# Zero-padded operands over all rows of the array, and weight chunks of half the size, in a two-block transformer kernel

## The chip, the core and the metric

The kernel runs on one core of a Trainium2 chip. A core has a matrix engine (TensorE, in the profile PE for its products and PEld for its loads of the stationary operand), VectorE (DVE), ScalarE (ACT), GpSimd (POOL) and SyncE (SP, which here only issues transfers). TensorE multiplies a stationary operand of up to 128 rows by 128 columns with a moving one of up to 512 columns. The metric is the device time of one execution in microseconds; lower is better.

## The reference, cut to what matters

Two transformer blocks of two layers each work on 512 tokens of 1024 features in float32. The first block has two SwiGLU feed-forward steps around a mixer of sliding-window attention (8 query heads, 2 key heads, window 128) and a convolution. The second block has a mixer of three parts (a gated delta rule, native sparse attention, stick-breaking attention) and a convolved feed-forward step. What the change touches are three products:

```python
# first block, sliding-window attention
s = jnp.einsum('bnqkgd,bnskd->bnkgqs', qb, kk) * (hd ** -0.5)
# second block, native sparse attention, selected and window keys
s_s = jnp.einsum('bqgrd,bgqnd->bgrqn', qb, k_sel) * scale
s_w = jnp.einsum('bqgrd,bngd->bgrqn', qb, kw) * scale
# second block, gated delta rule: q, k scaled per token
q = l2norm(to_chunks(q)) * D ** -0.5
k_beta = k * beta[..., None]
decay = jnp.exp(jnp.where(incl, g[..., :, None] - g[..., None, :], -jnp.inf))
```

A head has 64 features, so one head's queries or keys fill 64 of 128 partitions.

## The kernel before, in words

Activations are kept transposed: features on the 128 partitions, the 512 tokens along the columns. To keep float32 accuracy with the array's faster number format, each operand is split into a high and a low part, and a product of two tiles is three products (`mm3`, lines 259 to 261): high x high, high weight x low input, low weight x high input.

Weights come as chunks, in the order of use. `_fetch` (line 220) issues, on SyncE's queue, the transfers of the chunk that is wanted and the next ones, up to the `RAWS` = 3 buffers; a chunk is `CHUNK` = 8 tiles of 128 x 128, 512 KB. `_split_upto` casts half a chunk at a time, four tiles, to the high part on ScalarE (line 232) and subtracts for the low part on VectorE (line 233), `AHEAD` = 2 halves ahead of the products. A raw buffer is free again when its last half is split. In the second block's `compress` two whole chunks are used as they are (`wraw`).

The plan runs steps one after another: per layer of the first block a feed-forward step, `mixer1`, a feed-forward step and a gated embedding; per layer of the second block `mixer2`, `ffnc` and a gated embedding. A planner orders each engine's instructions from the program order, and lets an instruction that is ready pass one that still waits for a buffer.

In `mixer1` the products of the input come first; each of four convolution tiles is written to memory and read back four times, shifted (lines 478 and 482, SyncE's queue), into one of two buffers whose first columns GpSimd fills (line 480). Then, by query tile n, `scores(n + 1)` and `values(n)` alternate, and steps of the convolution (line 521) run beside them. A query tile `qs` holds [high, low] of one head on its 128 partitions, the key tile `ks` [high, high]; one product over all 128 rows (line 545) gives high x high plus low x high. The keys' low part is a second product over the 64 rows of the head (line 546), with `kl`, one tile for both key heads. VectorE takes the masked minimum from the score bank (line 549).

`mixer2` has the same pair in `nsa` (lines 1277 and 1278, tiles `kss`, `kws` and `ksl`, `kwl`). Its units of work are written out: the scores of unit u, then the transposes (line 1292) and the value products (line 266) of unit u - 2, then steps of the side work: output projection `pw`, the delta rule's scan, the compressed branch. The stages before it (`Gdn.pre`, `inverse`, `sb`) run with the remaining input products beside them. `pre` builds per-token factors as eight rows on partitions 0, 32 and 64 onwards, and `rows` (line 1514) spreads a group of eight over the partitions by a product with a selector `sel` of eight rows.

Of the kernel before, what the change touches and what calls it, by code (L numbers as in the profile page):

```python
# [10 lines left out]
F32 = mybir.dt.float32  # L11
# [7 lines left out]
T = 512  # L19
# [4 lines left out]
CHUNK = 8  # L24
AHEAD = 2
RAWS = 3
# [23 lines left out]
BLK = 16  # L50
SUB_RATE = 0.35
# [4 lines left out]
LAG = 4  # L56
# [9 lines left out]
class Vecs:  # L66
    """Column directory of the per-partition vectors."""
# [41 lines left out]
def const_layout():  # L109
    v = Vecs()  # L110
    for nm, n in (("tri", 128), ("last", 128), ("inc", 64), ("lev", 5 * 64), ("blk", 64), ("sub", 64), ("eye", BLK), ("hones", 2), ("high", 1), ("low", 1),
                  ("sbs", 128), ("cmask", 512), ("cmpm", 128), ("cmpn", 128)):
        v.add(nm, n)
    return v


class Net:
# [16 lines left out]
    def phase(self, **tags):  # L134
        """Scratch: rotating [128, 512] tiles, so many of each tag. Phases nest."""
# [8 lines left out]
    def psum(self, **tags):  # L144
        """PSUM banks, so many of each tag; or the tags that one goes round."""
# [41 lines left out]
    def setup(self):  # L187
# [5 lines left out]
        for i in range(8):  # L193
            nc.sync.dma_start(self.h[i], self.A["xT"][i * 128:(i + 1) * 128])
            if i in (0, 2, 4):
                self._fetch(i // 2, 1)
# [9 lines left out]
    def weights(self, sources):  # L206
        """The [128, 1024] chunks of all weights, in the order of use."""
# [7 lines left out]
    def _fetch(self, c, n=RAWS):  # L215
        for x in range(c, min(c + n, len(self.chunks))):
            if x not in self.rawt:
                r = self.raw.tile([128, CHUNK * 128], F32, tag="raw", name="raw")
                for f in (slice(0, 512), slice(512, 1024)) if x == 0 else (slice(None),):
                    self.nc.sync.dma_start(r[:, f], self.chunks[x][:, f])  # L220
                self.rawt[x] = r

    def _split_upto(self, h):
        nc = self.nc
        while self.nsplit <= min(h, 2 * len(self.chunks) - 1):
            c, half = divmod(self.nsplit, 2)
            if not self.israw[c]:
                self._fetch(c)
                r = self.rawt[c][:, half * 512:half * 512 + 512]
# [7 lines left out]
    def w(self):  # L237
        """The next 128-column tile of the weights."""
        h, o = divmod(self.at, CHUNK // 2)
# [6 lines left out]
    def wraw(self, n):  # L246
        """The next n chunks of the weights as they are."""
# [15 lines left out]
    def mm2(self, out, l, r, **flags):  # L263
        """A narrow product in two halves of its rows, side by side in the array."""
# [9 lines left out]
    def lin(self, name, xs, tag="lin"):  # L274
        """The next product."""
# [6 lines left out]
    def lead(self, name, n, tag="lin", gain=None, norm=None, at=8, between=None):  # L282
        """The input of a step, its first products side by side, and the norm of the input."""
# [51 lines left out]
    def rstd(self, tiles, n, scale=1.0, adds=SQ_DVE):  # L335
        """1/sqrt(mean(x^2)+eps) over the features of x = scale * tiles: a row on every partition."""
# [17 lines left out]
    def rn(self, acc, n, scale=1.0):  # L354
        """By token, 1/sqrt of the mean over the partitions."""
# [59 lines left out]
    def rope_tables(self, pos, inv, sgn):  # L415
        """cos and signed sin of pos * inv, features on partitions."""
# [24 lines left out]
    def rope(self, ps, cos, sin, half, tag="q", tmp="t"):  # L441
        """ps * cos + swap(ps) * sin, the swap within each 32 partitions."""
# [9 lines left out]
    def mixer1(self, i):  # L452
# [7 lines left out]
        # taps by fours: their weights on the diagonals of [4 x 32, 32], a group of 32 features after the other  # L460
# [8 lines left out]
        for j in range(4):  # L469
# [6 lines left out]
            # the tile's groups of 32 features, 0 to 3 tokens late  # L476
# [19 lines left out]
        # in parts, stacked: [high, low] of a head against [high, high] of its keys  # L496
        H = (slice(0, 64), slice(64, 128))
        kl, ks, qs = self.t(F32R, "kl", "q"), [], []
        for g in range(2):
            y = self.t(F32R, "ks", "q")  # L500
            for r in range(2):
                nc.scalar.copy(y[H[r]], kr[H[g]])
            nc.vector.tensor_tensor(kl[H[g]], kr[H[g]], y[H[g]].bitcast(F32), OP.subtract)
            ks.append(y)
        for j in range(4):
# [7 lines left out]
        def conv(j):  # L513
            """The convolution of tile j on the tensor engine, four taps at a time."""
# [18 lines left out]
        def scores(n):  # L533
# [4 lines left out]
            for g in range(2):  # L538
                for j in range(4):
# [6 lines left out]
                    last = nc.tensor.matmul(ps[:, f], q[H[g], b], kl[H[g], k], start=False, stop=True)  # L546
# [102 lines left out]
    def ple(self, pT, gain, norm, last=False):  # L649
        """The gate's product, and beside it the tokens' rms-normalised projection with its gain."""  # L650
# [46 lines left out]
    def final_out(self, gain, out):  # L697
        """The last norm, by token."""
# [38 lines left out]
    def pace(self, inst, **rates):  # L737
        """Steps of the work that runs beside the current one, so many of each kind, but not ahead of
        the instruction of LAG calls before."""
# [11 lines left out]
    def sparse(self, cost):  # L751
        """Small products of a cost were issued: as many large ones belong beside them."""
# [7 lines left out]
    def fill(self, kind, n=1):  # L760
        """n steps of a kind, or all that are left."""
# [11 lines left out]
    def need(self, done, kind):  # L773
        """Steps of a kind until done."""
# [9 lines left out]
    def by_token(self, y):  # L784
        """PSUM: the tokens of y on partitions, [token, (block, feature)]."""
# [5 lines left out]
    def mixer2(self, i, fin):  # L791
# [4 lines left out]
        st = self.t(name="st", tag="cd")  # L796
        nc.scalar.dma_start(st, self.A["sel"])
        sel = self.tp.tile([128, T], F32R, name="sel", tag="sel")
        nc.gpsimd.tensor_copy(sel, st)
# [105 lines left out]
    def norm2_in(self, i, fin):  # L905
        """The input of the second block's mixer; after the first block, its last norm too."""
# [4 lines left out]
        def gates(gain):  # L911
            """Their few columns in four groups, each a fourth of the features."""
# [13 lines left out]
        def norm():  # L926
# [13 lines left out]
            # of the two norms together: (mean of the second's square + eps) / first's^2  # L940
# [9 lines left out]
    def rsqrt_ln(self, x, n, scale):  # L950
        """1/sqrt(scale * x + eps): exp of the logarithm, and one Newton step."""
# [10 lines left out]
    def head_norm(self, *args):  # L962
        """out = src / rms(src) over each 64 columns."""
# [16 lines left out]
    def to_mix(self, o, nt):  # L980
        """A token block, transposed."""
# [937 lines left out]
```

## Time and profile before

| | us |
|---|---|
| time, median of 3 runs | 3790.53 |
| lowest and highest of the runs | 3789.84, 3797.76 |
| span of the profiled execution, first to last instruction | 3791.1 |

The times are of whole executions. For the profiled one only its span is on record; it lies 0.6 us above the median of the runs, so 3791.1 us serves as its own time. In the profile, "busy" counts an engine's own instructions; a TensorE product is listed with its start and a modelled length, and since products overlap, its cost is read from one start to the next. In the operand column `64*128` is 64 rows by 128 columns of the array in use, `64x256` the moving operand. The granted clock is 1.00 at 2.4 GHz and 0.50 at 1.2 GHz.

### The profile page before, as it was taken

What the parts mean: (1) busy time and instruction counts of PE and PEld (TensorE: products, weight loads), DVE (VectorE), ACT (ScalarE), POOL (GpSimd) and SP (SyncE); (2) the same over time, 40 slices, a digit from 0 to 9 for tenths busy, and PEclk for the clock granted to TensorE, in tenths of its full rate; (3) what the DMA queues carried; (4) which work ended last, traced back from release to release, by engine and by line L of the source; (5) the groups of instructions that cost most, each with busy time, mean ns of one, the idle gap of its engine ahead of it and who ended that gap; (6) DMA issues with size and microseconds to landing.
All of it is one profiled execution on the core that took longest, in us unless ns stands there. A gap on an engine that the chain in (4) does not pass through costs nothing. (4 is left out here: it accounts for less than half of the span.)

```text
span 3791.1 us, 53948 instructions
## 1 busy us (share of the span) xinstructions
PE 3723.9 (98%) x20946; PEld 2919.5 (77%) x20946; DVE 2311.5 (61%) x4820; ACT 1563.9 (41%) x2974; POOL 147.2 (4%) x150
## 2 busy tenths in 40 slices
PE   9999999999999999999999999999999999999998
PEld 7888757888888885688887777778887777778887
DVE  5445556444743445753448876675667786676667
ACT  4233344333532334532345344553445344554345
POOL 1000000000100000100001000000001000000001
PEclk9999999999999998999999998999999999999999
DMA  3223312222322242122232111122323111122232
GB/s 132 99 95 101 106 40 89 95 100 95 100 95 100 95 127 64 52 98 100 95 100 94 68 40 68 40 100 95 100 95 134 51 40 62 46 90 100 95 100 84
DMA packets 97152, 329.85 MB, mean 87 GB/s; under 512 B 11008, under 2 KB 14976, under 8 KB 96896
## 3 DMA queue, kind: packets, MB, share of 16 engines
q1 hardware_dynamic: 90144, 311.96, 24.9%
q10 hardware_dynamic: 5472, 10.25, 0.8%
q0 software_dynamic: 1280, 4.20, 0.3%
q8 instruction: 164, 2.69, 0.3%
q14 instruction: 92, 0.75, 0.1%
HBM read 317.97 MB, written 8.39 MB: 86 GB/s over the span
## 5 line engine op out<-in xcount | busy, mean ns | idle before, releaser
L232 ACT CAST wH<-raw 128x512 fp32r<-128x512 f32 x1116 | 691.3, 620 | 1421.9 <-PE pgu L260 451.2
L233 DVE TENSOR_TENSOR wL<-raw,wH 128x512 fp32r<-128x512 f32 x1116 | 791.2, 710 | 590.4 <-ACT wH L232 558.2
L259 PE MATMUL pgu<-xH,wH 128*128 128x512 f32 x1408 | 549.5, 391 | 9.7 <-ACT wH L232 5.9
L260 PE MATMUL pgu<-xL,wH 128*128 128x512 f32 x1408 | 551.2, 391 | 6.1 <-DVE xL L313 6.1
L261 PE MATMUL pgu<-xH,wL 128*128 128x512 f32 x1408 | 550.7, 391 | 0.0
L259 PE MATMUL pd<-H,wH 128*128 128x512 f32 x1056 | 410.8, 389 | 0.0
L260 PE MATMUL pd<-L,wH 128*128 128x512 f32 x1056 | 410.8, 389 | 0.0
L261 PE MATMUL pd<-H,wL 128*128 128x512 f32 x1056 | 410.8, 389 | 0.0
L259 PEld LDWEIGHTS pgu<-xH,wH 128*128 128x128 f32 x1408 | 265.3, 188 | 65.2 <-ACT wH L232 5.9
L260 PEld LDWEIGHTS pgu<-xL,wH 128*128 128x128 f32 x1408 | 266.3, 189 | 62.2 <-DVE xL L313 6.7
L261 PEld LDWEIGHTS pgu<-xH,wL 128*128 128x128 f32 x1408 | 266.2, 189 | 55.4 <-DVE wL L233 0.2
L259 PE MATMUL pup<-xH,wH 128*128 128x512 f32 x704 | 274.8, 390 | 2.2 <-DVE h L895 1.2
L261 PE MATMUL pup<-xH,wL 128*128 128x512 f32 x704 | 274.0, 389 | 0.0
L260 PE MATMUL pup<-xL,wH 128*128 128x512 f32 x704 | 273.9, 389 | 0.0
L260 PEld LDWEIGHTS pd<-L,wH 128*128 128x128 f32 x1056 | 198.2, 188 | 41.1
L259 PEld LDWEIGHTS pd<-H,wH 128*128 128x128 f32 x1056 | 198.2, 188 | 41.1
L261 PEld LDWEIGHTS pd<-H,wL 128*128 128x128 f32 x1056 | 198.2, 188 | 41.1
L348 POOL TENSOR_TENSOR ssum<-ssum,sq 128x512 f32<-128x512 f32 x72 | 110.6, 1536 | 2674.7 <-ACT sq L347 2673.3
L259 PEld LDWEIGHTS pup<-xH,wH 128*128 128x128 f32 x704 | 132.1, 188 | 31.5 <-DVE h L895 2.0
L261 PEld LDWEIGHTS pup<-xH,wL 128*128 128x128 f32 x704 | 132.1, 188 | 27.6
L260 PEld LDWEIGHTS pup<-xL,wH 128*128 128x128 f32 x704 | 132.1, 188 | 27.1
L1344 DVE SCALAR_TENSOR_TENSOR y<-x,vecs,y 128x511 f32<-128x511 f32 (+1 forms) x176 | 131.3, 750 | 17.1 <-ACT y L1341 14.3
(568 smaller groups left out, 6108.0 us busy)
## 6 DMA issues: line engine op xcount, KB each, us to landing
raw<-ffn SPq DMA_DIRECT2D x395, 512.0 KB, 3.2
raw<-w_in SPq DMA_DIRECT2D x82, 512.0 KB, 3.2
raw<-w_out SPq DMA_DIRECT2D x40, 512.0 KB, 3.2
raw<-w_ple_gate SPq DMA_DIRECT2D x40, 512.0 KB, 3.2
away<-h ACTq DMA_DIRECT2D x16, 256.0 KB, 2.1
raw<-cmp SPq DMA_DIRECT2D x8, 512.0 KB, 3.3
h<-away POOLq DMA_DIRECT2D x16, 256.0 KB, 5.1
h<-xT SPq DMA_DIRECT2D x8, 256.0 KB, 6.5
```

Source lines behind the costliest of these rows:

```text
L232: nc.scalar.copy(H, r)
L233: nc.vector.tensor_tensor(L, r, H.bitcast(F32), OP.subtract)
L259: nc.tensor.matmul(ps, w[0], x[0], start=first, stop=False)
L260: nc.tensor.matmul(ps, w[0], x[1], start=False, stop=False)
L261: nc.tensor.matmul(ps, w[1], x[0], start=False, stop=last)
L348: (nc.vector if k >= adds else nc.gpsimd).tensor_tensor(acc, acc, q, OP.add)
L1344: nc.vector.scalar_tensor_tensor(y[:, s:], x[:, :T - s], w[:, f * 3 + tap:f * 3 + tap + 1], y[:, s:], OP.mult, OP.add)
```

## The change

- Each key head gets a low-part tile of its own with zeros in the other head's 64 partitions, filled by GpSimd, and the low-part products take all 128 rows of the query tile: the other 64 rows meet zeros.
- The factor rows are products over 96 rows: `sel` has five blocks of 128 columns with ones only in the rows of one factor, and the moving operand is the whole of `RS`. `sel` grows from 512 to 640 columns and comes in two transfers.
- A weight chunk is 4 tiles, 256 KB, in 4 buffers instead of 8 tiles in 3. A split takes a whole chunk. The transfers at the start follow one after each of the first four tiles of the input; `compress` takes four chunks.
- Scratch: one more tile for `mixer1`, two more for `mixer2`; of the five level masks of the triangular inverse only the one in use stays.
- Comments and doc strings are dropped.

```diff
-CHUNK = 8
+CHUNK = 4
-RAWS = 3
+RAWS = 4
+LEVELS = tuple(range(BLK.bit_length() - 1, 5))
...
-            if i in (0, 2, 4):
-                self._fetch(i // 2, 1)
+            if i < RAWS:
+                self._fetch(i, 1)
...
-                for f in (slice(0, 512), slice(512, 1024)) if x == 0 else (slice(None),):
+                for f in (slice(0, 256), slice(256, 512)) if x == 0 else (slice(None),):
...
-        while self.nsplit <= min(h, 2 * len(self.chunks) - 1):
-            c, half = divmod(self.nsplit, 2)
+        while self.nsplit <= min(h, len(self.chunks) - 1):
+            c = self.nsplit
             if not self.israw[c]:
                 self._fetch(c)
-                r = self.rawt[c][:, half * 512:half * 512 + 512]
+                r = self.rawt[c]
...
@@ mixer1
-        kl, ks, qs = self.t(F32R, "kl", "q"), [], []
+        kl, ks, qs = [], [], []
         for g in range(2):
-            y = self.t(F32R, "ks", "q")
+            y, low = self.t(F32R, "ks", "q"), self.t(F32R, "kl", "q")
+            nc.gpsimd.memset(low[H[1 - g]].bitcast(F32), 0.0)
             for r in range(2):
                 nc.scalar.copy(y[H[r]], kr[H[g]])
-            nc.vector.tensor_tensor(kl[H[g]], kr[H[g]], y[H[g]].bitcast(F32), OP.subtract)
+            nc.vector.tensor_tensor(low[H[g]], kr[H[g]], y[H[g]].bitcast(F32), OP.subtract)
             ks.append(y)
+            kl.append(low)
...
-                    last = nc.tensor.matmul(ps[:, f], q[H[g], b], kl[H[g], k], start=False, stop=True)
+                    last = nc.tensor.matmul(ps[:, f], q[:, b], kl[g][:, k], start=False, stop=True)
@@ mixer2
-        st = self.t(name="st", tag="cd")
-        nc.scalar.dma_start(st, self.A["sel"])
-        sel = self.tp.tile([128, T], F32R, name="sel", tag="sel")
-        nc.gpsimd.tensor_copy(sel, st)
+        sel = self.tp.tile([128, 640], F32R, name="sel", tag="sel")
+        for f in (slice(0, 512), slice(512, 640)):
+            st = self.t(name="st", tag="cd")[:, :f.stop - f.start]
+            nc.scalar.dma_start(st, self.A["sel"][:, f])
+            nc.gpsimd.tensor_copy(sel[:, f], st)
@@ nsa_split, keys (ks and kw)
-            low = d[nm + "l"] = self.t(F32R, nm + "l", "gs")
+            d[nm + "l"] = []
             for g in range(2):
-                y = self.t(F32R, nm + "s", "gs" if nm == "ks" else "v")
+                y, low = self.t(F32R, nm + "s", "gs" if nm == "ks" else "v"), self.t(F32R, nm + "l", "gs")
+                nc.gpsimd.memset(low[H[1 - g]].bitcast(F32), 0.0)
...
+                d[nm + "l"].append(low)
@@ nsa, scores
-            nc.tensor.matmul(ps, q[s, b], d[key + "l"][s, :w], start=False, stop=True)
+            nc.tensor.matmul(ps, q[:, b], d[key + "l"][g][:, :w], start=False, stop=True)
@@ compress
-            W = self.wraw(2)
+            W = self.wraw(4)
@@ Gdn.pre
-        def rows(p, base, blk, f=lambda x: x):
-            nc.tensor.matmul(p, self.sel[base:base + 8, blk], f(RS[base:base + 8]), start=True, stop=True)
+        def rows(p, which, f=lambda x: x):
+            nc.tensor.matmul(p, self.sel[:96, which * 128:which * 128 + 128], f(RS[:96]), start=True, stop=True)
...
-        nc.vector.tensor_tensor(kb, k, rows(N.pat("row"), 32, B), OP.mult)
+        nc.vector.tensor_tensor(kb, k, rows(N.pat("row"), 3), OP.mult)
...
@@ build
-                        with n.phase(cd=4, gq=5, gs=4, gp=12, gat=3, v=4), tc.tile_pool(name="sp2", bufs=1) as n.sp2:
+                        with n.phase(cd=4, gq=5, gs=6, gp=12, gat=3, v=4), tc.tile_pool(name="sp2", bufs=1) as n.sp2:
-                            with n.phase(q=14, qt=2, S=8, t=2, p=2, o=3, c=8, cp=4):
+                            with n.phase(q=15, qt=2, S=8, t=2, p=2, o=3, c=8, cp=4):
```

## Rows read from the trace of the kernel before

**Rows 1.** The profile's page, part 1: busy us (share of the span) xinstructions.

```profile
PE 3723.9 (98%) x20946; PEld 2919.5 (77%) x20946; DVE 2311.5 (61%) x4820; ACT 1563.9 (41%) x2974; POOL 147.2 (4%) x150
```

**Rows 2.** A down projection's products: stretch, length, busy us (xcount), clock, DMA share, GB/s.

```profile
720.50:779.50 59.00, 58.96 (x261) 48.84 (x262) 4.83 (x7) 1.00 0.28 97
```

**Rows 3.** Busy time by stretch: the four attention stages.

```profile
452.00:542.00 90.00, 88.85 (x596) 37.89 (x594) 39.89 (x158) 39.33 (x129) 0.21 (x2) 0.85 0.12 30
...
1457.00:1543.00 86.00, 84.75 (x594) 37.17 (x595) 39.41 (x157) 38.66 (x129) 0.21 (x2) 0.86 0.13 32
...
2306.00:2460.00 154.00, 152.98 (x1342) 107.27 (x1341) 93.45 (x308) 77.35 (x219) 1.10 (x5) 0.91 0.13 42
...
3188.00:3330.00 142.00, 141.19 (x1330) 101.00 (x1328) 91.50 (x307) 74.49 (x214) 1.09 (x5) 0.98 0.14 46
```

**Rows 4.** Order of time on TensorE (start us, us): full products, second block.

```profile
2192.42 0.34 PE L1182 MATMUL sbz<-SL,cr 128*128 128x384 f32 x1
2192.59 0.40 PE L1182 MATMUL sbz<-SHL,cr 128*128 128x256 f32 x2
2192.83 0.22 PE L1182 MATMUL sbz<-SH,cr 128*128 128x128 f32 x1
```

**Rows 5.** Order of time on TensorE: a score unit of the second block.

```profile
2386.81 0.34 PE L1277 MATMUL pss<-kss,q0s 128*128 128x384 f32 x1
2387.08 0.43 PE L1278 MATMUL pss<-ksl,q0s 64*128 64x384 f32 x1
2387.44 0.44 PE L1292 MATMUL ppt<-ident,S 128*128 128x128 f32 x2
```

**Rows 6.** Order of time on TensorE: scores of the first block.

```profile
490.20 0.38 PE L545 MATMUL sc<-ks,qs 128*128 128x256 f32 x1
490.51 0.38 PE L546 MATMUL sc<-kl,qs 64*128 64x256 f32 x1
490.82 0.39 PE L545 MATMUL sc<-ks,qs 128*128 128x256 f32 x1
```

**Rows 7.** Order of time on TensorE: factor rows of the delta rule.

```profile
2081.05 0.73 PE L1514 MATMUL row<-RS,sel 8*128 8x512 f32 x3
2081.71 0.50 PE L260 MATMUL pqkv<-xL,wH 128*128 128x512 f32 x1
2082.05 0.39 PE L261 MATMUL pqkv<-xH,wL 128*128 128x512 f32 x1
2082.37 0.49 PE L1514 MATMUL row<-RS,sel 8*128 8x512 f32 x1
2082.79 0.50 PE L259 MATMUL pqkv<-xH,wH 128*128 128x512 f32 x1
```

**Rows 8.** One line's instructions: count, duration ns min/median/max, first and last start us.

```profile
L546 PE MATMUL sc<-kl,qs x64: 322/382/579, 452.7 to 1516.2; 64*128 64x256 f32 x48, 64*128 64x128 f32 x16
...
L1278 PE MATMUL pss<-ksl,q0s x16: 323/435/579, 2306.7 to 3301.9; 64*128 64x128 f32 x4, 64*128 64x256 f32 x4, 64*128 64x384 f32 x4, 64*128 64x512 f32 x4
...
L1514 PE MATMUL row<-RS,sel x24: 383/496/501, 2081.0 to 3052.4; 8*128 8x512 f32 x24
```

**Rows 9.** Waits from 452 to 516 us: total us, times, longest us.

```profile
POOL u L480 <- PE pc L521: 137.6, 2, 112.2
...
PEld sc L545 <- DVE nm L549: 4.7, 5, 1.6
```

**Rows 10.** DMA issues: out<-in engine op xcount, KB each, median us to landing.

```profile
raw<-ffn SPq DMA_DIRECT2D x395, 512.0 KB, 3.2
```

**Rows 11.** Order of time on SyncE, which issues the weights, first mixer.

```profile
396.21 2.08 SPq L478 DMA_DIRECT2D um<-ca  x2
...
403.20 0.38 SPq L220 DMA_DIRECT2D raw<-w_in  x1
...
483.95 27.22 SPq L482 DMA_DIRECT2D u<-um  x8
```

**Rows 12.** Busy time by stretch: one spell at the lower clock.

```profile
455.00:482.00 27.00, 26.82 (x77) 10.38 (x77) 9.70 (x42) 10.42 (x41) 0.00 (x0) 0.50 0.00 1
```

More of the change, by code (lines that the diff above doesn't have):

```diff
@@ L110, in const_layout @@
     v = Vecs()
-    for nm, n in (("tri", 128), ("last", 128), ("inc", 64), ("lev", 5 * 64), ("blk", 64), ("sub", 64), ("eye", BLK), ("hones", 2), ("high", 1), ("low", 1),
+    for nm, n in (("tri", 128), ("last", 128), ("inc", 64), ("lev", 64 * len(LEVELS)), ("blk", 64), ("sub", 64), ("eye", BLK), ("hones", 2), ("high", 1), ("low", 1),
                   ("sbs", 128), ("cmask", 512), ("cmpm", 128), ("cmpn", 128)):
@@ L237, in w @@
     def w(self):
-        h, o = divmod(self.at, CHUNK // 2)
+        h, o = divmod(self.at, CHUNK)
         if o == 0:
@@ L1103, in compress @@
             for l in range(16):
-                wl = W[l // 8][:, (l % 8) * 128:(l % 8 + 1) * 128]
+                wl = W[l // CHUNK][:, l % CHUNK * 128:(l % CHUNK + 1) * 128]
                 o, f = (0, 2 * l) if l < 8 else (1, 16 + 2 * l)
@@ L1269, in scores @@
             g, r, w = hd // 3, hd % 3, (n + 1) * 128
-            s, b = slice(g * 64, g * 64 + 64), slice(n * 128, n * 128 + 128)
+            b = slice(n * 128, n * 128 + 128)
             if hd == 0:
@@ L1511, in pre @@
         yield
-        def rows(p, base, blk, f=lambda x: x):
-            nc.tensor.matmul(p, self.sel[base:base + 8, blk], f(RS[base:base + 8]), start=True, stop=True)
+        def rows(p, which, f=lambda x: x):
+            nc.tensor.matmul(p, self.sel[:96, which * 128:which * 128 + 128], f(RS[:96]), start=True, stop=True)
             return p
-        A, B = slice(0, 128), slice(256, 384)
         kb = self.kb[j]
-        nc.vector.tensor_tensor(kb, k, rows(N.pat("row"), 32, B), OP.mult)
-        nc.vector.tensor_tensor(k, k, rows(N.pat("row"), 64, A), OP.mult)
+        nc.vector.tensor_tensor(kb, k, rows(N.pat("row"), 3), OP.mult)
+        nc.vector.tensor_tensor(k, k, rows(N.pat("row"), 4), OP.mult)
         yield
         self.qe[j] = self.room[j][1]
-        nc.vector.tensor_tensor(self.qe[j], q, rows(N.pat("row"), 32, A), OP.mult)
-        nc.vector.tensor_tensor(q, q, rows(N.pat("row"), 0, A), OP.mult)
+        nc.vector.tensor_tensor(self.qe[j], q, rows(N.pat("row"), 2), OP.mult)
+        nc.vector.tensor_tensor(q, q, rows(N.pat("row"), 0), OP.mult)
         yield
@@ L1532, in pre @@
         yield
-        pg = rows(N.pat("pg"), 0, B)
+        pg = rows(N.pat("pg"), 1)
         dt = self.t(name="dt", tag="gd")
@@ L1537, in pre @@
         nc.scalar.activation(dt, dt, AF.Exp)
-        pe = rows(N.pat("pel")[:, :8], 0, B, lambda x: x[:, 63::64])
+        pe = rows(N.pat("pel")[:, :8], 1, lambda x: x[:, 63::64])
         self.egl[j] = N.sp2.tile([128, 8], F32, name="el", tag="el", bufs=3)
@@ L1560, in lev @@
         def lev(l):
-            return N.con2("lev")[:, l * 64:(l + 1) * 64].unsqueeze(1).to_broadcast([128, 8, 64])
+            return N.con2("lev")[:, (l - LEVELS[0]) * 64:(l - LEVELS[0] + 1) * 64].unsqueeze(1).to_broadcast([128, 8, 64])
         def gi(name):
@@ L1591, in inverse @@
         N.pace(step, **rates)
-        for l in range(BLK.bit_length() - 1, 5):
+        for l in LEVELS:
             p = gi("px")
@@ L1865, in host @@
     con("lev", np.concatenate([(r // (2 * m) == c64 // (2 * m)) & (r // m % 2 == 1) & (c64 // m % 2 == 0)
-                               for m in (1, 2, 4, 8, 16)], 1))
+                               for m in (2 ** l for l in LEVELS)], 1))
     con("blk", r // BLK == c64 // BLK)
@@ L1883, in host @@
     con("low", lower)
-    S = np.zeros((128, 512), np.float32)
-    for c, h in ((0, 0), (1, 1)):
-        for r in (0, 32, 64, 4, 36, 68):
-            S[r + h, c * 64:c * 64 + 64] = 1
-    for c, h in ((2, 0), (4, 0), (5, 1), (7, 1)):
-        for r in (2, 34, 6, 38):
-            S[r + h, c * 64:c * 64 + 64] = 1
+    S = np.zeros((128, 640), np.float32)
+    for which, row in enumerate((0, 2, 32, 34, 64)):
+        for h in range(2):
+            for r in (row + h, row + h + 4):
+                S[r, which * 128 + h * 64:which * 128 + h * 64 + 64] = 1
     A["sel"] = S
```

## The prediction, on record before the result

> **What bounds the kernel now.** I read the page's busy times first: TensorE is busy 98% of the span, VectorE 61%, ScalarE 41%, GpSimd 4% [rows 1]. A busy TensorE is not yet a TensorE at its peak, so the next view is the busy time by stretch. In a down projection of a feed-forward step 261 products of 512 columns fill 59.0 us, 0.226 us from start to start, at a granted clock of 1.00 [rows 2]. That is the kernel's dense pace: 59.0 / 261. The four attention stretches look different [rows 3]. TensorE is just as busy there, but the granted clock is 0.85, 0.86, 0.91 and 0.98, and no other engine is near its limit: VectorE has 40 of 90 us and 94 of 154 us. So in these stages, too, it is TensorE's order of work that sets the end, and a shorter order should show in the span.
>
> Then the order of time on TensorE, which gives the cost of one product as the distance from its start to the next start. Products that use all 128 rows, one behind the other, take 0.17 us at 384 columns (2192.42 to 2192.59) and 0.12 us at 256 (two from 2192.59 to 2192.83) [rows 4]. A low-part product of the second block has 64 rows. With it, the pair of 384 columns takes 2386.81 to 2387.08, 0.27 us, and 2387.08 to 2387.44, 0.36 us, though nobody waits for data there [rows 5]. In the first block's attention a string of pairs of 256 columns runs at 0.31 us per product, both ways (490.20, 490.51, 490.82) [rows 6]. So what costs time is the change between a product over 64 rows and one over 128: about 0.10 us (0.27 - 0.17) before the 64-row product and 0.19 us (0.36 - 0.17, 0.31 - 0.12) behind it. The factor rows, with 8 rows, show the same: 2082.05 to 2082.37 is 0.32 us, 0.09 over the pace, and 2082.37 to 2082.79 is 0.42 us, 0.19 over it [rows 7].
>
> **The change part by part.** *Second block's scores.* Line 1278 runs 96 times, in six groups of 16 by query and key tile, of which one is shown [rows 8]. Each becomes a product over all rows. It has as many columns, so it should cost its pace, and both changes vanish if its neighbours are full, as the transposes behind it are [rows 5]: 0.10 + 0.19 = 0.29 us, over 96 products 28 us. Where a value product or a product of the scan (64 columns or rows of the array) comes next, the array is changed there anyway and only the first 0.10 us is saved; if that were so everywhere, the gain would be 10 us. Most are followed by a transpose or a large product, since the order puts the transposes of two units earlier right behind the scores, so I take 21 us, about a quarter off the upper end, and keep 10 to 28.
>
> *First block's scores.* Line 546 runs 64 times [rows 8]. Inside a string both products of the pair lose 0.19 us, 0.38 us a pair, 24 us at most; where the convolution (32 columns of the array) or the values come next only 0.19 us, 12 us at least. Half and half gives 18 us. Here something else is late next: VectorE's masked minimum frees the score banks, and TensorE already waits 4.7 us for it in five places of one layer [rows 9]. I take a third off: 12 us, bounds 5 and 24. These strides are those at the higher clock; at the lower one the changes cost more, which the upper bound covers.
>
> *Factor rows.* Line 1514 makes 24 row products [rows 8]. One that stands alone saves 0.09 + 0.19 = 0.28 us. But three issued together take 0.66 us in all (2081.05 to 2081.71), that is 0.22 us each, because products over different rows of the array run beside each other; over all rows they take 3 x 0.226 = 0.68 us [rows 7]. So the grouped ones save about nothing. The Trainium skill, "TensorE: Matmul & The Clock Gate", section "Why this matters for your kernels", says of products with few rows that they should be laid on distinct row groups so that they run at once, which speaks against widening them; by that rule, with all 24 in pairs that share one product's time, widening them adds 12 x 0.226 = 2.7 us. The trace bears the rule out for the grouped rows only; the low-part products have no partner to run beside. With half of the 24 alone the term is 12 x 0.28 = 3 us, with bounds of -3 (all of them sharing) and 6 (all alone). The other products of this line are few and I count nothing for them.
>
> *What is added.* Two half-tile fills per first mixer and four per second one, twelve in all, on GpSimd, which is busy 4% [rows 1]; the keys that they complete also wait for two ScalarE copies and a VectorE subtraction, so I cost them at nothing. If that cover were gone, each first use of a key tile would wait; the third rival prices it. The selector gets a second small transfer and a second conversion on GpSimd at the start of each second mixer, long before its first use; the constants beside it shrink by four of five level masks. Nothing.
>
> *Weight chunks.* A chunk is 512 KB and lands 3.2 us after its issue [rows 10]. The casts and subtractions keep their shape of 512 columns, so ScalarE and VectorE do the same work. What changes is how far the loads run ahead: three chunks of eight tiles are 24 tiles, four chunks of four are 16. Four tiles are 12 products, 2.7 us at the dense pace, so 16 tiles are 10.9 us, and with a landing of at most 3.2 us over 7 us are to spare in the dense stages. The place to look at is the first mixer, where SyncE issues no weights from 396.21 to 403.20, 7.0 us, because the convolution's copies hold its queue [rows 11]. The shorter lead is worth 8 tiles, 5.4 us, so at worst each of the two layers starves for 5.4 us, 11 us in all; the lead of 10.9 us is longer than the hold, so I take 1 us.
>
> *The clock.* Half speed, 1.2 GHz instead of 2.4, held without a break from 455 to 482 [rows 12]. From the granted clocks of the four stretches the time at the lower level is 2 x (1 - clock) x length: 27, 24, 28 and 6 us, 85 us in all [rows 3]. At half speed 85 us cost 42 us at most. All four lie where the scores start with their narrow products. The last two are the same program on the same shapes, once with 28 us and once with 6, so the stage stands near the edge where the level changes. With the pauses gone the same columns pass in less time, which should bring the higher level sooner, but the first scores will also wait more for VectorE. I take 6 us, bounds -11 (the fourth as long as the third: half of 22) and 42.
>
> The sum: 21 + 12 + 3 - 1 + 6 = 41 us. The profiled execution spans 3791.1 us, within 1 us of the median of 3790.5, so 3791.1 - 41 = 3750 us.
>
> **The rivals.** *The clock comes back as well.* If the longest three low stretches shrink to the 6 us of the fourth, 61 us less at the lower level give 30 us instead of 6, and with full score terms the time is about 3791 - 66 = 3725, down to 3706. For it speaks the fourth stretch; against it, that the first mixer's two spells are alike (27 and 24 us) and start at the same place. The Trainium skill, the same page's Part 1, has activity release the throttle from a half-speed default, which would favour this one.
>
> *The gain goes into waits.* TensorE gets through the scores faster but then stands for VectorE's minimum and the exponentials; only the second half of the second block's stage, where the large products of the output projection lie between the scores, gives its share: 10 + 5 = 15 us, 3776. For it: the 4.7 us of waits [rows 9]. Against it: VectorE is busy less than two thirds of every one of these stretches [rows 3].
>
> *The fills stand behind a blocked queue.* GpSimd's fill of a convolution buffer waits up to 112.2 us for the convolution to free it [rows 9]. If the key fills are queued behind it, the first block's low-part scores cannot start before that buffer is free, when the copies into it go out at 483.95 [rows 11], instead of at 452.7 [rows 8]: up to 31 us in each of two layers, 62 us, less the 41, a time of about 3812. It decides from 21 us a layer. Against it: SyncE's order shows later weights issued ahead of the blocked copies [rows 11], so the order lets ready work pass.
>
> *It does nothing.* The time lies in the narrow products themselves and not in the change of rows: 3791. The full products of equal width at 0.12 and 0.17 us [rows 4] speak against it.
>
> **How the numbers follow.** Forecast, 25 to 60 us less: 0.62. Clock as well, 60 to 85 us less: 0.15. Into waits, 8 to 25 us less: 0.12. Nothing: 0.04. Slower by the fills, or by starving weights: 0.07. A measurement of this kernel can tell about 0.2%, 7.6 us, from no change. Faster: 0.62 + 0.15 + 0.12 = 0.89; same 0.04; slower 0.07. For the range I leave out the nothing and slower cases and the outer ends of the two beside the forecast: 3706 to 3777.
>
> **What the profile after would show.** Right: the pairs of rows 5 and 6 at 0.17 and 0.12 us a product, with 128 rows on both; the second block's score stages 9 to 13 us shorter each, the first's 5 to 9 us; casts that wait for TensorE and not for a load. Wrong: strides that stay at 0.3 us on full rows; score products waiting for VectorE by as much as they were shortened; GpSimd's fills late; a pause between products of the first mixer before 420 us; low-clock stretches longer than before. The largest doubt is the clock, then how much of the first block's 18 us VectorE lets through.

## The result, and the profile after

| | before | after |
|---|---|---|
| median of the runs, us | 3794.15 (4 runs, 3789.84 to 3799.39) | 3724.24 (4 runs, 3721.87 to 3727.08) |
| span of the profiled execution, us | 3791.1 | 3725.3 |
| mean granted TensorE clock | 0.984 | 0.993 |

The ratio is 0.982, 95% interval 0.9804 to 0.9836: faster by 1.8%. The median lies inside the range on record and 26 us below the predicted point of 3750. A second measurement of the same kernel, beside the experiments, gave 0.9815 (0.9794 to 0.9836).

Busy time, as in [rows 1]. TensorE stays at 98% and is busy 70 us less with the same 20946 products; GpSimd, with its fills, is busy 9 us more:

```profile
PE 3654.2 (98%) x20946; PEld 2902.1 (78%) x20946; DVE 2307.7 (62%) x4820; ACT 1563.1 (42%) x2974; POOL 155.9 (4%) x164
```

The four attention stages by stretch, with the columns of [rows 3]. They are shorter, and the clock has risen in each: from 0.85, 0.86, 0.91 and 0.98 to these.

```profile
452.00:528.00 76.00, 72.74 (x593) 32.59 (x594) 39.14 (x158) 38.33 (x130) 0.23 (x2) 0.96 0.16 37
1443.50:1518.00 74.50, 72.48 (x596) 32.94 (x594) 38.99 (x158) 38.16 (x128) 0.23 (x2) 0.93 0.16 38
2281.00:2411.00 130.00, 128.93 (x1337) 99.24 (x1336) 91.07 (x306) 76.64 (x217) 1.11 (x5) 1.00 0.17 50
3139.00:3266.00 127.00, 125.53 (x1329) 97.73 (x1329) 90.50 (x307) 74.90 (x214) 1.10 (x5) 1.00 0.19 51
```

The order of time on TensorE in the second block, for the unit of [rows 5]. The pair of 384 columns goes at 0.17 us for the first product and 0.18 for the second, against 0.27 and 0.36 before:

```profile
2346.45 0.34 PE L1283 MATMUL pss<-kss,q0s 128*128 128x384 f32 x1
2346.62 0.34 PE L1284 MATMUL pss<-ksl,q0s 128*128 128x384 f32 x1
2346.80 0.38 PE L1298 MATMUL ppt<-ident,S 128*128 128x128 f32 x2
```

The same view in the first block, for the string of [rows 6]. Both products of a pair start 0.12 us apart, against 0.31:

```profile
480.07 0.28 PE L548 MATMUL sc<-ks,qs 128*128 128x256 f32 x1
480.19 0.28 PE L549 MATMUL sc<-kl,qs 128*128 128x256 f32 x1
480.31 0.28 PE L548 MATMUL sc<-ks,qs 128*128 128x256 f32 x1
```

The factor rows, as in [rows 7]. Three together take 2058.81 to 2059.59, 0.78 us, which is more than the 0.66 of the 8-row form; the single one takes 0.34 instead of 0.42, and the product ahead of it 0.24 instead of 0.32:

```profile
2058.81 0.94 PE L1520 MATMUL row<-RS,sel 96*128 96x512 f32 x3
2059.59 0.40 PE L261 MATMUL pqkv<-xL,wH 128*128 128x512 f32 x1
2059.83 0.39 PE L262 MATMUL pqkv<-xH,wL 128*128 128x512 f32 x1
2060.07 0.50 PE L1520 MATMUL row<-RS,sel 96*128 96x512 f32 x1
2060.41 0.39 PE L260 MATMUL pqkv<-xH,wH 128*128 128x512 f32 x1
```

The waits of the first mixer's attention, 452 to 503 us, with the columns of [rows 9]. TensorE and its loads now wait 8.3 us for VectorE's minimum (5.6 and 2.7), against 5.8 before (4.7 and 1.1). GpSimd's blocked fill `u` is still there. The first line is of before, the others of after:

```profile
PE sc L545 <- DVE nm L549: 1.1, 1, 1.1
```

```profile
POOL u L481 <- PE pc L524: 123.7, 2, 101.5
...
PEld sc L548 <- DVE nm L552: 5.6, 5, 1.9
...
PE sc L548 <- DVE nm L552: 2.7, 3, 1.8
```

GpSimd's order of time. The two key fills come at 371.97, a hundred microseconds ahead of the fill of 474.53, whose wait for the convolution stands in its bracket. So the key fills wait behind nothing:

```profile
371.97 1.10 POOL L502 MEMSET kl<- 64x512 f32 x2
474.53 0.11 POOL L481 MEMSET u<- 128x12 f32 x1 [101.46 <-PE pc L524]
```

A chunk of half the size lands in 2.6 us, against 3.2 in [rows 10]:

```profile
raw<-ffn SPq DMA_DIRECT2D x791, 256.0 KB, 2.6
```

In the first mixer, where the lead was feared to be too short, ScalarE's casts do wait for a load:

```profile
412.50 1.27 ACT L233 CAST wH<-raw 128x512 fp32r<-128x512 f32 x2 [5.30 <-DMA raw<-w_in]
414.41 0.62 ACT L233 CAST wH<-raw 128x512 fp32r<-128x512 f32 x1 [0.64 <-DMA raw<-w_in]
```

TensorE filled that gap with 24 products of the convolution, which before stood a little later (at 416.50). The products of the next tile, `pk`, which come behind both, start at 419.46:

```profile
413.89 2.76 PE L524 MATMUL pc<-u,cd 128*32 128x512 f32 x24
...
419.46 0.39 PE L260 MATMUL pk<-xH,wH 128*128 128x512 f32 x1
```

Before, they started at 419.19. The starved loads cost 0.3 us at most in this layer.

### The profile page after: what moved, and what is told of

It reads as the page before. It is cut to its first block, busy times and chain, and to the rows that moved or that the text cites. A ratio compares the mean times of both kernels' runs of the same rounds, so it can differ in the third digit from the quotient of the medians.

```text
span 3725.3 us, 55291 instructions
## 1 busy us (share of the span) xinstructions
PE 3654.2 (98%) x20946; PEld 2902.1 (78%) x20946; DVE 2307.7 (62%) x4820; ACT 1563.1 (42%) x2974; POOL 155.9 (4%) x164
```

## The experiments

Stage lengths below go by the first product of one kind to the first of another: the first mixer from `pag` to `pA`, the score stage of the second block from `pss` to `pup`. "Low" is time at 1.2 GHz inside the stage.

Three theories. One: the change from 64 rows to 128 and back costs the time, and strings of such changes also go with the low clock. Two: it is the half-filled array during the low-part products that goes with the low clock, and the number of changes does not matter for it. Three: the spells at the low clock come by chance, and the wide score products give only their direct time.

**Both blocks' low products on 64 rows, the rest of the change kept.**

```diff
-last = nc.tensor.matmul(ps[:, f], q[:, b], kl[g][:, k], start=False, stop=True)
+last = nc.tensor.matmul(ps[:, f], q[H[g], b], kl[g][H[g], k], start=False, stop=True)
...
-nc.tensor.matmul(ps, q[:, b], d[key + "l"][g][:, :w], start=False, stop=True)
+nc.tensor.matmul(ps, q[s, b], d[key + "l"][g][s, :w], start=False, stop=True)
```

> The changed kernel with only the low-part score products of both blocks put back on the 64 rows of their head; padded tiles, chunks and factor rows stay. Theory 1 (each change between 64 and 128 rows stops the array, and the stops bring the clock down): the strides of 0.31 us return, the low-clock time in the four attention stages goes from 17 back to about 85 us, time 3785 to 3795 us, mean clock about 0.984. Theory 2 (the half-filled products, not the stops, bring the clock down) expects the same here. Theory 3 (the clock's spells are chance and only the strides changed): about 3755 us, clock between 0.984 and 0.993. If the smaller chunks had part in the gain, the time stays more than 8 us below the kernel before.

3773.79 us, ratio 0.9936 (0.9912 to 0.9961), clock 0.988. Of the 70 us gained 50 are gone by the medians and 44 by the ratios: the low clock of the first mixer is back (27 and 24 us), that of the second block's score stage is not (0 and 0). The time lies between the 3785 to 3795 of theories one and two and the 3755 of three; the low time is 51 us, not the 85 that the first two expected.

**Only the first block's on 64 rows** (the first of the two edits).

> Only the first block's low-part products back on 64 rows. Theories 1 and 2: the first block's two attention stages return to 90 and 86 us of length, from 76 and 75, so about 25 us above the changed kernel, 3750 us, with about 50 us of low clock there and none in the second block's score stages. Theory 3: about 9 us above, 3733 us.

3747.11 us, 0.9867 (0.9837 to 0.9897). The first mixers are back at 170.5 and 166.8 us, with 24 us of low clock in each; the score stages stay short, 153.5 and 152.7. The median fits the 3750 of theories one and two, but the profile is of the slowest of four executions, and the fastest, 3737.75 at a clock of 0.992, lies near the 3733 of theory three.

**An eight-column product of 64 rows ahead of each of the 160 wide pairs**, overwritten by the pair.

```diff
+nc.tensor.matmul(ps[:, f][:, 0:8], q[H[g], b], kl[g][H[g], k][:, 0:8], start=True, stop=True)
 nc.tensor.matmul(ps[:, f], q[:, b], ks[g][:, k], start=True, stop=False)
...
+nc.tensor.matmul(ps[:, 0:8], q[s, b], d[key + "l"][g][s, 0:8], start=True, stop=True)
 nc.tensor.matmul(ps, q[:, b], d[key + "s"][g][:, :w], start=True, stop=False)
```

> The changed kernel, with all low-part products on all rows, and ahead of each of the 160 score pairs one product more, of 64 rows and only 8 columns, whose output is overwritten: the changes of rows return without any half-filled work to speak of. At 0.10 us before and 0.17 us behind each, 30 to 43 us come directly. Theory 1: the clock falls as well, the low time in the attention stages rises from 17 to 60 us or more, time 3775 to 3800 us. Theory 2: the clock stays at about 0.993, time 3754 to 3767 us.

3784.86 us, 0.9967 (0.9953 to 0.9982), clock 0.987: 61 us above the changed kernel by the medians, 56 by the ratios, 57 by the spans of the profiles. The price of the change alone, on TensorE in the second layer's mixer:

```profile
1467.10 0.27 PE L548 MATMUL sc<-kl,qs 64*128 64x8 f32 x1
1467.30 0.39 PE L549 MATMUL sc<-ks,qs 128*128 128x256 f32 x1
1467.52 0.28 PE L550 MATMUL sc<-kl,qs 128*128 128x256 f32 x1
1467.73 0.27 PE L548 MATMUL sc<-kl,qs 64*128 64x8 f32 x1
```

The eight-column product takes 0.20 us to the next start (1467.10 to 1467.30), the wide product behind them takes 0.22 (to 1467.52) and the one ahead of the next eight 0.21 (to 1467.73), instead of 0.12 each. In this string a pair costs 0.63 us instead of 0.24, so the eight columns cost 0.39 in all. Elsewhere a neighbour is narrow anyway or TensorE waits for VectorE: with low time taken at the 0.41 us per us worked out below, the four attention stages are 41 us longer than the changed kernel's, 0.26 us for each of the 160. The other 15 to 20 us go with the clock (99 us of low time in the whole execution, against 57), though almost no column was added on half the rows. In the four stages the low time is 51 us, against 17; theory one had asked for 60 or more. All ten executions had a clock of 0.985 to 0.990. Theory two, with 0.993 and 3754 to 3767 us, falls.

**First block on 64 rows, ordered high, high, low, low within each score bank.** The same products are issued, but in this order the score sums are not the right ones (probably part of one head's sum in each bank is lost; no run shows it). So the run tells times and is no kernel to use.

```diff
+for _, _, f, q in pair:
+    nc.tensor.matmul(ps[:, f], q[:, b], ks[g][:, k], start=True, stop=False, ...)
+for _, _, f, q in pair:
+    last = nc.tensor.matmul(ps[:, f], q[H[g], b], kl[g][H[g], k], start=False, stop=True, ...)
```

> As first_back, but the two pairs of a score bank are issued as full, full, low, low, so that the 64-row products come two by two and half of the changes go. Theory 1: of the roughly 9 us that the changes cost directly about half comes back and the low-clock time falls with them: 8 to 14 us below first_back. Theory 2: as many half-filled columns as in first_back, so its low-clock time, and only 3 to 6 us below it.

3726.32 us, 0.9814 (0.979 to 0.9837): 21 us below the ungrouped form, more than theory one (8 to 14) and theory two (3 to 6) expected, and as fast as the wide products. On TensorE four products now take 0.86 us (1461.34 to 1462.20), 0.215 each, between the 0.31 of [rows 6] and the 0.12 of the wide form:

```profile
1461.34 0.50 PE L553 MATMUL sc<-ks,qs 128*128 128x256 f32 x2
1461.77 0.50 PE L555 MATMUL sc<-kl,qs 64*128 64x256 f32 x2
1462.20 0.50 PE L553 MATMUL sc<-ks,qs 128*128 128x256 f32 x2
```

128 products by 0.095 us are 12 us at most. All four executions had a clock of 0.992, and the ungrouped one that had it as well was 11 us slower (3737.75), so the direct part holds. The rest of the 21 goes with the clock: in the profiles the low time of the two first mixers fell from 48 to 17 us. Half the changes and the same number of half-filled columns speak for theory one; but two later profiles with ungrouped narrow scores have 14 and 3 us there, so this run alone does not decide between one and two.

**The changed kernel once more, and with the factor rows on 8 rows.**

> The changed kernel once more, unaltered, as the standard for the runs beside it on the same chip. It was 3724 us (3722 to 3727); the same within 5 us is expected, with the same 57 us of low clock within 15.

> The changed kernel with the delta rule's factor rows as products over 8 rows again, and nothing else altered. By the working on record the wide factor rows are worth 3 us (bounds -3 and 6), so 3 us above the changed kernel. The rival: three grouped 8-row products share the array's time, so the wide form gains nothing or loses up to 3 us, and this kernel is equal or up to 3 us faster. A third: the factor rows' changes of rows also hold the clock down, as the score products' do, and the low-clock spells near 2073 and 2107 us return (10 us at half speed, 5 us of time).

3722.7 us (0.9815) and 3729.62 us (0.9833, interval 0.9811 to 0.9854): 7 us, more than the 3 on record. The repeat met its expectation. The clock is not the answer: the low time of a whole execution is 57 us with 8 rows, and 57 and 65 in the two profiles with 96, whose spans lie only 2 to 3 us below. To find where, I added up over all factor products the time from the start of the product ahead to the end of the group, where the next product starts. The 24 of tile `row` take 10.7 us with 8 rows and 10.2 with 96: nothing to speak of. The twelve others of the same line, the decays `pg` and the eight-column `pel`, bring the sum for all 36 from 18.7 to 16.1 us. One of these with 8 rows, and one with 96:

```profile
2058.99 0.40 PE L261 MATMUL pqkv<-xL,wH 128*128 128x512 f32 x1
2059.32 0.27 PE L1519 MATMUL pel<-RS,sel 8*128 8x8 f32 x1
2059.52 0.50 PE L262 MATMUL pqkv<-xH,wL 128*128 128x512 f32 x1
```

```profile
2064.66 0.40 PE L261 MATMUL pqkv<-xL,wH 128*128 128x512 f32 x1
2064.89 0.18 PE L1520 MATMUL pel<-RS,sel 96*128 96x8 f32 x1
2064.93 0.48 PE L262 MATMUL pqkv<-xH,wL 128*128 128x512 f32 x1
```

0.53 us from the product ahead to the one behind against 0.27: the eight-column product saves as much as a lone one of 512 columns (0.74 against 0.47 in four of six places). So 2.6 us are direct, as the spans have it; the other four of the seven are near what these runs can tell, and I leave them open.

**Half-size chunks alone, on the kernel before.**

> The kernel before with the weight chunks of four tiles in four buffers, and nothing else of the change. If the clock in the second block's score stage hangs on the changes of rows alone, its low stretches there stay (27 and 7 us), the clock stays at 0.98, and the time is that of the kernel before, up to 2 us more. If the smaller chunks decide where that stage starts and so whether its spell comes, the stretches are gone as in the run with both blocks' low products on 64 rows, the clock is 0.988, and the time is 3775 to 3785.

3789.46 us, 0.9999 (0.9986 to 1.0012). The chunks cost nothing and bring nothing. The low time of the score stages is 10 us in each here, where the kernel before has 27 and 10, with no product changed.

**Wide factor rows alone, on the kernel before.**

> The kernel before with the wide factor rows and their longer selector, and nothing else of the change. Direct term: the stretch between the second block's first product and its score stage, with the low time taken at half, was 2.7 and 1.3 us longer with 8-row factor rows than without, so 4 us, a ratio of 0.999. If the factor rows' changes of rows also bring the low clock of the score stage behind them (27 and 10 us in the kernel before), that is gone too, another 10 to 17 us: a ratio of 0.995 and a clock 0.004 higher.

3781.87 us, 0.9977 (0.9964 to 0.9989): 9 us, between the two expectations. The low time of the score stages was 14 and 7 us, so it had not gone. This kernel also has the four level masks fewer, so the 9 us are not the factor rows' for certain.

**Scores and factor rows both narrow again** (chunks, zero-filled tiles and their room kept), **and the first experiment again beside it.**

> The changed kernel with the score products on 64 rows and the factor rows on 8 rows again: what is left of the change is the chunks, the zero-filled tiles and their room. Chunks alone gave a ratio of 0.9999, the run with only the score products back 0.9936. If the 24 us between these two are the factor rows' (directly and by the clock), this kernel gives 0.999 to 1.000 and the low stretches of the score stage return; if they come from the fills, the extra buffers or the order that follows from them, it gives 0.994.

> The run with only the score products on 64 rows once more, unaltered, as the standard for the two beside it: a ratio of 0.9936 within 0.002 and no low clock in the score stage, if the 24 us between it and the chunks alone are a property of the kernel; a ratio nearer to 1 if they were that execution's or that chip's.

0.9971 (0.996 to 0.9982) and 0.9947 (0.9933 to 0.9962). The repeat met its expectation (within 0.002, and 0 us of low time in both score stages). The kernel with both kinds narrow meets neither of its two: the factor rows account for 9 of the 24 us that were asked about (20 by the repeat), and about 10 remain in a kernel that has neither kind of wide product. One of its score stages had 38 us of low time, the other none. The repeat also shows how much of such a difference is one execution's. It is the program of the first experiment, and its 975 products of the second layer's first mixer took 166.78 us at a clock of 0.93 in one profile (first fence) and 158.47 us at 0.99 in the other (last row of the second fence; its first two rows are the score stages):

```profile
1376.94:1543.72 166.78, 165.53 (x975) 101.06 (x973) 90.19 (x257) 67.70 (x177) 1.41 (x6) 0.93 0.30 80
```

```profile
2292.36:2457.26 164.90, 160.58 (x1476) 118.02 (x1474) 112.05 (x343) 90.17 (x246) 8.34 (x15) 1.00 0.19 55
3163.58:3325.81 162.23, 157.75 (x1469) 116.71 (x1468) 111.24 (x343) 88.63 (x243) 7.83 (x10) 1.00 0.19 55
1372.35:1530.82 158.47, 157.17 (x975) 98.31 (x973) 90.18 (x257) 67.56 (x177) 1.41 (x6) 0.99 0.32 84
```

That is the price of the clock with nothing else in it: 2 x 0.07 x 166.78 - 2 x 0.01 x 158.47 = 20.2 us less at half speed bring 8.3 us, 0.41 us for each. The next pair gives the same.

**Half-size chunks and the scratch of the changed kernel, none of its wide products.**

> The run with the chunks alone, with the scratch of the changed kernel besides (one more tile in the first mixer, two more in the second, one level mask instead of five), without its zero-filled tiles, wide scores or wide factor rows. The run with everything but the wide products gave a ratio of 0.9971, the chunks alone 0.9999. If the 10 us between them come from the buffers (keys that wait for a free tile ahead of the score stage), this gives 0.997 and the clock 0.986; if from the filled tiles and the order that they bring, 0.9995 to 1.000 and 0.984.

3777.06 us, 0.9959 (0.9944 to 0.9975). Three more scratch tiles and four constants fewer are worth 15 us over the chunks alone. The same stage of the second layer, with chunks alone and then with the room:

```profile
1376.40:1543.20 166.80, 165.55 (x976) 101.19 (x974) 90.25 (x257) 67.86 (x177) 0.36 (x4) 0.93 0.30 80
```

```profile
1373.20:1531.60 158.40, 157.10 (x976) 98.41 (x974) 90.15 (x257) 67.56 (x177) 0.36 (x4) 0.99 0.32 84
```

TensorE issues the 975 products of this stage in the same order in both, reaches the first score after 81.1 us in both, and waits 1.1 us at the same place. The long low spell begins 4 us after the first score product in the one (1461.6) and not at all in the other, where a short one comes at 1470.0, 16 us after it. So it is not this order that the room changed. The twelve runs of this kernel went from 3769.42 us at a clock of 0.992 to 3797.9 at 0.981, the ten with chunks alone only from 0.986 down to 0.982. The ratio fits the expectation of 0.997 roughly, but its reason, keys that wait for a free tile, is not what the trace shows: around the head of the first score stage (2290 to 2340 us) TensorE waits 0.6 us in all with chunks alone, and not at all with the room. Whether it is the tiles or the masks no run separates.

**More products widened by zeros:** the stick-breaking scores, with a key tile per head, and the compressed branch's second value product.

```diff
-nc.tensor.matmul(p, d["sk"][j][s, b * 128:(b + 1) * 128], d["sq"][j][s, b * 128:], start=True, ...
+nc.tensor.matmul(p, d["sk"][j][hd % 2][:, b * 128:(b + 1) * 128], d["sq"][j][:, b * 128:], start=True, ...
...
-nc.tensor.matmul(po[:, 256:384], ct[:64, 128:256], vm[:64, 256:384], start=True, stop=True)
+nc.tensor.matmul(po[:, 256:384], ct[:, 128:256], vm[:, 256:384], start=True, stop=True)
```

> The changed kernel with two more kinds of products widened to all rows by zeros: the stick-breaking scores (32 products of 64 rows, each key tile in two copies, one a head, the other half zero) and the compressed branch's second value product (8 of 64 rows). If the price of changing rows holds there too, 0.29 us x 40 = 11.6 us at most, so 3713 us, clock up a little; if VectorE, busy for 78% of the time in that stage and with four more halves to write in a layer, sets its end, the time stays at 3724; at worst the added VectorE work is on the path, 4 x 0.6 us in each of two layers, 3729.

3720.18 us, 0.9808 (0.9787 to 0.9829): 2.5 us below the changed kernel beside it, a difference inside the intervals, and between the 3713 and the 3724 expected. By the spans of the profiled executions, 3717.4 against 3726.1 and 3725.3, it is 8 to 9 us, and from start to start the 32 stick-breaking scores take 15.0 us instead of 23.6. All its runs had a clock of 0.992, where the changed kernel's had 0.992 to 0.994. It is the lowest median of the study; the products are cheaper, but the whole kernel is not shown to be faster.

## Why the prediction was right, and what it mis-sized

The profiled executions lie 65.8 us apart (3791.1 to 3725.3); the sum on record was 41. So the case with the chance of 0.62, 25 to 60 us less, is not what was measured. The range holds because it takes in the rival with the clock, which had 0.15.

**Second block's scores, 21 predicted, 24 measured.** The pair that shows it without the clock is the repeated experiment above, with both score stages at 1.00, and the changed kernel, whose score stages are these, also at 1.00:

```profile
2281.32:2434.47 153.15, 148.09 (x1475) 116.38 (x1474) 111.08 (x343) 90.35 (x246) 8.34 (x15) 1.00 0.20 59
3139.06:3289.10 150.04, 144.60 (x1470) 114.96 (x1468) 110.35 (x343) 88.95 (x243) 7.84 (x10) 1.00 0.21 59
```

164.90 - 153.15 is 11.8 us, 162.23 - 150.04 is 12.2. Each stage lies inside the 9 to 13 us that were to show it right. But the 0.29 us for one product leaves out a third share: the wide product behind a 64-row one pays as well. The unit of [rows 5] ran from 2386.81 to 2387.64 before, with its two transposes, and runs from 2346.45 to 2346.93 now, 0.35 us less:

```profile
2387.64 0.48 PE L259 MATMUL pw<-mH,wH 128*128 128x512 f32 x1
```

```profile
2346.93 0.48 PE L260 MATMUL pw<-mH,wH 128*128 128x512 f32 x1
```

For 96 products that would be 34 us, and 24 came, so the part to take off for narrow neighbours was larger than a quarter. That the two errors nearly cancel in the 21 is luck.

**First block's scores, 12 predicted, 12 measured.** The wide form of the second layer's first mixer at a clock of 1.00 is in the profile with 8-row factor rows, a kernel that differs from the changed kernel only in a later stage:

```profile
1363.87:1514.80 150.93, 148.77 (x975) 95.53 (x973) 89.71 (x257) 67.36 (x177) 1.41 (x6) 1.00 0.33 89
```

Against it stand 158.47 us with narrow scores and 3 us of low time, 1.3 us by the price above: 157.2 - 150.9 = 6.3. In the first layer 165.4 us with 14 us low against 157.0 with 7, so 159.7 - 154.1 = 5.6. The waits for VectorE did grow, by 2.5 us in one layer, which was the reason for taking a third off, 3 us a layer.

**Factor rows, 3 predicted, 2.6 direct.** The sum was right and its parts were not. Six of the 24 row products stand alone, not half. Those on which it counted, the row products, gave 0.4 us, since the wide groups of two and three lost what the single ones won. The Trainium skill, "TensorE: Matmul & The Clock Gate", section "Why this matters for your kernels", would have products with few rows side by side on distinct row groups; the trace agrees for these groups, which with 8 rows took 0.66 us for three and 0.43 for two, and with 96 rows 0.78 and 0.57. The twelve on which it counted nothing, as "few", gave 2.2. Whoever counts changes must count the shortest products too.

**Chunks, -1 predicted, 0 measured** (0.9999). One sign on record went wrong here: casts were to wait for TensorE and not for a load. In each first mixer they wait for a load twice, and it costs 0.3 us at most, because the convolution had products ready.

**The clock, 6 predicted, 27 measured.** This is the term that was mis-sized and nearly the whole miss. 65.8 - 24 - 12 - 2.6 leaves 27. It can be had another way: 2 x (1 - 0.984) x 3791 = 121 us at half speed before, 2 x (1 - 0.993) x 3725 = 52 after, 69 less, and 69 x 0.41 is 28. The step on record reckoned that shorter stages with more waits would give back little of the 85 us in the attention stages. By the trace they fell to 17. The rival named "the clock comes back as well", 3725, is what happened; its place, the long stretches of the attention stages, is right too.

Where those 27 us come from is settled in part. Low time in the stages, over all the profiles of this study, in us per stage:

| | first layer, first mixer | second layer, first mixer | score stages |
|---|---|---|---|
| narrow scores (8 profiles; 7 for the score stages) | 14 to 27 | 24 in five, 3 in three | 0 to 38 |
| wide scores (4 profiles; 6 for the score stages) | 7 to 10 | 0 to 10 | 0 to 10 |

(The run with the first block alone narrow counts as wide in the last column, and so does the grouped one, which is in neither row of the first two, with 17 and 0. The run with the extra eight-column products is in no row: 14, 10, 0 and 27.) With wide scores no profile has a long spell; with narrow ones it comes in some executions and not in others, of one and the same program. Shown: taking the changes away removes the long spells, and putting only the changes back, without half-filled columns, brings the clock down. The four runs with all scores wide had 0.991 to 0.994 in all their 17 executions, the kernel with the eight-column products 0.985 to 0.990 in all ten. Shown as well: the room and the missing masks by themselves raised it, with the order of the products unchanged, by about 15 us in time (11 in the run with both kinds narrow again). So of the 27 us the changes account for some 12 to 16, by this difference. Theory one holds for the long spells; theory three has this much in it, that with narrow scores they come in some executions only, and that a part goes with something that no edit of the scores touches. Why the room does it is open: the spells begin at other products there, and what sets that wasn't found.

**The rivals that failed.** Fills behind a blocked queue (3812): the fills run 100 us before the blocked one. Gain into waits (3776): the waits of one layer grew from 5.8 to 8.3 us, and the four stages shrank by 11 to 23. It does nothing (3791): 0.12 and 0.17 us, as worked out.

## What to carry to other kernels

Read the price of a narrow product from one start to the next, together with that of its wide neighbours: here 0.10 us on the wide product ahead of a 64-row one, about 0.19 on the 64-row one itself and 0.10 on the wide one behind it, whether it has 8 columns or 384, and padding with zeros took all of it away at no cost on TensorE. Grouping the narrow products two by two halved the number of changes and came out as fast, but in an order that spoils the sums; one that keeps them was not run. And a stretch at the lower clock is not a fixed property of a kernel: take its price from two profiles of one program, give it a range as wide as that, and repeat a run before explaining why a spell is missing.

## What the runs showed that was not expected

- The half-speed time had a price of 0.41 us per us in these stages, not 0.5. In the run with chunks alone a low-part product of 256 columns takes 0.51 us to the next start at the lower clock (1465.51 to 1466.02), against 0.31 at the higher: with a pace doubled from 0.12 to 0.24, what the change of rows adds goes from 0.19 to 0.27, which is less than double.
- One program's runs, twelve of them, spread over 28 us with the mean granted clock from 0.992 to 0.981, about 2.6 us for each 0.001.
- A product of 96 rows is not quite a product of 128: the single factor row of [rows 7]'s kind still took 0.34 us to the next start, 0.11 over the dense pace, in two of its six places (0.23 to 0.24 in the others).
- The stick-breaking scores are float32 products and stand in the trace as two records each. With 64 rows both records cost more than with 128, in the changed kernel and in the one with more padding:

```profile
L1175 PE MATMUL sbz<-sq,sk x64: 272/481/693, 2146.4 to 3108.0; 64*128 64x128 f32 x16, 64*128 64x256 f32 x16, 64*128 64x384 f32 x16, 64*128 64x512 f32 x16
```

```profile
L1179 PE MATMUL sbz<-sq,sk x64: 271/483/697, 2141.3 to 3097.1; 128*128 128x128 f32 x16, 128*128 128x256 f32 x16, 128*128 128x384 f32 x16, 128*128 128x512 f32 x16
```

The listed durations (min/median/max) are nearly the same and hide it; from start to start a pair of 128 columns took 0.42 us with 64 rows (0.214 + 0.201) in all eight places, and with 128 rows 0.14 (0.109 + 0.031) in the two shortest of eight and up to 0.39 beside products that do not fill the array.
